# An encoder kernel whose opening runs the first gate earlier and whose queries are transposed in float32, two heads at a time

## The chip, the cores and the metric

The kernel runs on one core of a Trainium2 chip. TensorE (PE) multiplies matrices into PSUM banks, VectorE (DVE) and ScalarE (ACT) do elementwise work, GpSimd (POOL) small parts of it, and SyncE (SP) issues the loads of the weights. The metric is the device time of one execution in microseconds (us), the median of several.

## The reference

Two layers of an encoder on 256 tokens of width 1024, in float32. Each layer is a half-step FFN, a mixing block with two attentions, and a second half-step FFN:

```python
x = x + 0.5 * swiglu(rms_norm(x, ffn1_norm[l]), ffn1_w_gate[l], ffn1_w_up[l], ffn1_w_down[l])
h = rms_norm(x, mix_norm[l])
z = h @ w_in[l]
qa, ka, va, qs, ks_, vs, zg = jnp.split(z, splits, axis=-1)
qa = rms_norm(qa.reshape(B, S, NA_HEADS, NA_HEAD_DIM), na_q_norm[l])
...
o_na = neighbourhood_attention(qa, ka, va, na_rpb[l])
...
o_sw = sliding_window_gqa(qs, ks_, vs, t5_bias, sw_sink[l])
g = jax.nn.sigmoid((zg + b_gate[l]).astype(jnp.float32)).astype(x.dtype)
merged = g[:, :, 0] * (o_na @ w_branch_na[l]) + g[:, :, 1] * (o_sw @ w_branch_sw[l])
x = x + merged @ w_out[l]
x = x + 0.5 * swiglu(rms_norm(x, ffn2_norm[l]), ffn2_w_gate[l], ffn2_w_up[l], ffn2_w_down[l])
```

where `swiglu` is `(silu(x @ w_gate) * (x @ w_up)) @ w_down` with a hidden width of 2816.

## The kernel before

**Products.** The 256 tokens are two tiles t of 128. Every float32 operand is split into a rounded part hi (wh, xh: float32r, a copy on ACT) and a rest lo (wl, xl: a subtraction on DVE); `split_to` (L183) does both. `three` (L169) then makes one product of three matmuls, hi x hi, hi x lo, lo x hi. One such step with 512 columns is the unit of the program's own clock: `tick` counts steps, and `defer` puts a piece of work into the order a given number of steps later.

**Orders.** TensorE's order is the order of the program, with the deferred pieces in between. The order of the other engines is made by a scheduler when the kernel is built. The exception is the opening: `linked` (L124) ties each ACT and DVE instruction that is emitted through it behind the one before on that engine, until `chain.clear()`. A piece of weights is one load of 512 KB into one of four buffers raw, then a split wh on ACT and wl on DVE; a buffer raw is free for the next load when wl has read it.

**Opening** (L225 to 271, once, in layer 0's first FFN). The first chunk of gate and up weights, 512 columns in four pieces, is multiplied while x is still being transposed and split, for both tiles, in the banks ps_g (tag "g", two of them). Then come squares of x for the norm (`square`, L214; after the second half of a tile, GpSimd makes rs_y from it) and the pieces of the second chunk. The gate of a chunk, Silu on ACT (sg, L453) and a product on DVE (hh, L454), reads the bank of its tile and so frees it for the next chunk. The gate of the first chunk's tiles is emitted behind the whole opening, outside of the tied order.

**Queries** (L492 to 506). `queries` norms one tile of queries: z and its square on ACT, the sums hv on DVE, the root rs_y on GpSimd, the product qn on DVE (`normed`, L479). It splits qn into qs, 8 heads of [hi | lo], 128 columns each. 16 steps later `turn` transposes the eight heads with the float32r unit matrix ident_r into two banks tp (tag "tp", two of them), and ACT copies each bank into qT (or sqT): hi in partitions 0 to 63, lo in 64 to 127. The calls are Q0 and Q1 (sliding window, tiles 0 and 1), q1 and q0 (neighbourhood). `keys` (L508) does the like for K0, K1 and k0, k1, with the same head twice in a row of kn and the split after the transposes.

**Attention** (L531 to 603). Per head, `front` multiplies scores sc, then makes the softmax: S with its minimum mx on DVE, Exp on ACT, a scaling of S by GpSimd (L571). `turn` transposes S into the one bank pt, and ACT and DVE split it into ph and pl; `back` multiplies by the values into the one bank po. These are deferred by P_LAG and V_LAG, and by MORE for single heads. The bias of a head comes from t5b (sliding window) or is made by GpSimd as b from a load t (neighbourhood, L665). The string ORDER (L47) names what is projected when, and, as a5 and the like, how many steps later a head's scores come.

## Time and profile before

| | us |
|---|---|
| median of 3 runs | 1078.03 (1077.65 to 1078.95) |
| the profiled execution | 1077.96 |
| its span in the trace | 1076.2 |
| first matmul of the second chunk, behind the opening | starts at 21.21 |
| query transposes of layer 0 | 208.75, 216.30, 227.59, 234.73 |
| query transposes of layer 1 | 740.99, 748.54, 759.84, 766.98 |

Times in the trace count from the start of the span; 1.76 us of the execution lie around it. A row of a timeline gives start, length, engine, line, operation, what is written from what, and the count where several were merged. L502 is line 502 of the kernel before.

### The profile page before, as it was taken

The numbers are of one execution on the slowest core, as the hardware profiler recorded it, in microseconds if no ns is written. First come the engines' busy times: TensorE is split into PE (matmuls) and PEld (weight loads), VectorE is DVE, ScalarE is ACT, GpSimd is POOL, SyncE is SP. The second block draws the span as 40 slices with busy tenths as digits, with TensorE's granted clock in tenths as the row PEclk, the third lists the DMA queues.
The fourth block names the chain that finished last, engine by engine and source line by source line (L and its number), as shares of the span: only waits on it lengthen the run. The fifth ranks groups of instructions, "written<-read, shape, count | busy, mean of one in ns | idle before, by whom it ended". The sixth has DMA issues, their size and how long they took to land.

```text
span 1076.2 us, 14744 instructions
## 1 busy us (share of the span) xinstructions
PE 1069.2 (99%) x5125; PEld 890.2 (83%) x5125; DVE 875.9 (81%) x1337; ACT 671.6 (62%) x1014; POOL 116.9 (11%) x118
## 2 busy tenths in 40 slices
PE   9999999999999999999999999999999999999998
PEld 6888888888888888888878888888888888888887
DVE  5688898889886768879877888988898867778795
ACT  6565754788764556565465665557877646566562
POOL 1000030243520000000000000003534000000000
PEclk9999999999999999999999999999999999999999
DMA  8667665765654667756657766648666555776562
GB/s 259 214 217 237 211 206 176 227 199 151 195 184 137 202 201 241 244 167 193 208 160 232 235 210 206 183 150 242 181 196 180 181 173 161 236 232 204 197 196 78
DMA packets 98828, 212.63 MB, mean 198 GB/s; under 512 B 7569, under 2 KB 13745, under 8 KB 98753
## 3 DMA queue, kind: packets, MB, share of 16 engines
q1 hardware_dynamic: 98560, 211.60, 62.4%
q8 instruction: 40, 0.66, 0.2%
q14 instruction: 36, 0.29, 0.1%
q0 software_dynamic: 192, 0.08, 0.1%
HBM read 210.59 MB, written 1.06 MB: 197 GB/s over the span
## 4 chain that ended last, share of the span: by engine, by line
PE 95%; DVE 2%; ACT 1%; issue 1%; DMA 0%
PE g L170 22%; PE g L172 22%; PE g L171 22%; PE acc L170 5%; PE acc L172 5%; PE acc L171 5%; PE tp L318 2%; PE sc L558 1%; PE po L593 1%; PE tp L170 1%; PE tp L172 1%; PE pt L579 1%; PE tp L171 1%; DVE wl L185 1%; PE tp L201 1%
## 5 line engine op out<-in xcount | busy, mean ns | idle before, releaser
L185 DVE TENSOR_TENSOR wl<-raw,wh 128x1024 fp32r<-128x1024 f32 x336 | 404.6, 1217 | 67.8 <-ACT wh L184 65.2
L184 ACT ACTIVATE wh<-raw 128x1024 fp32r<-128x1024 f32 x336 | 346.7, 1045 | 129.4 <-DMA raw<-in_w_gu 47.8
L170 PE MATMUL g<-wh,xh 128*128 128x512 f32 (+1 forms) x976 | 383.8, 393 | 0.8 <-DVE hh L454 0.8
L172 PE MATMUL g<-wh,xl 128*128 128x512 f32 (+1 forms) x976 | 377.8, 387 | 0.7 <-DVE xl L185 0.7
L171 PE MATMUL g<-wl,xh 128*128 128x512 f32 (+1 forms) x976 | 377.4, 387 | 0.0
L172 PEld LDWEIGHTS g<-wh,xl 128*128 128x128 f32 x976 | 183.4, 188 | 40.0 <-DVE xl L185 2.1
L170 PEld LDWEIGHTS g<-wh,xh 128*128 128x128 f32 x976 | 183.6, 188 | 33.9 <-DVE hh L454 1.2
L171 PEld LDWEIGHTS g<-wl,xh 128*128 128x128 f32 x976 | 183.7, 188 | 32.7
L453 ACT ACTIVATE sg<-g,rs_y 128x256 f32<-128x256 f32 x88 | 41.0, 466 | 91.1 <-PE g L172 78.7
L454 DVE SCALAR_TENSOR_TENSOR hh<-g,rs_y,sg 128x256 f32<-128x256 f32 x88 | 42.1, 479 | 54.0 <-ACT sg L453 53.9
L170 PE MATMUL acc<-wh,hi 128*128 128x512 f32 x180 | 71.1, 395 | 0.0
L172 PE MATMUL acc<-wh,lo 128*128 128x512 f32 x180 | 70.2, 390 | 0.0
L171 PE MATMUL acc<-wl,hi 128*128 128x512 f32 x180 | 70.1, 389 | 0.0
L176 POOL TENSOR_TENSOR rs_y<-ms,mhalf 128x1 f32<-128x1 f32 x12 | 6.7, 554 | 553.5 <-DVE ms L222 545.1
L350 DVE TENSOR_TENSOR u<-raw 128x512 f32<-128x512 f32 x64 | 41.9, 685 | 15.2 <-DMA raw<-in_w_d 15.0
L184 ACT ACTIVATE corner<-raw 128x512 fp32r<-128x512 f32 x32 | 20.2, 631 | 50.1 <-DMA raw<-in_w_d 33.0
L571 POOL TENSOR_TENSOR S<-S,sm 128x512 f32<-128x512 f32 x32 | 37.1, 1160 | 65.7 <-DVE sm L570 38.3
L172 PEld LDWEIGHTS acc<-wh,lo 128*128 128x128 f32 x180 | 33.8, 188 | 7.2
L171 PEld LDWEIGHTS acc<-wl,hi 128*128 128x128 f32 x180 | 33.8, 188 | 6.8
L170 PEld LDWEIGHTS acc<-wh,hi 128*128 128x128 f32 x180 | 33.8, 188 | 6.7
L564 ACT ACTIVATE S<-S,mx 128x256 f32<-128x256 f32 x64 | 31.9, 500 | 8.0 <-DVE mx L561 7.9
L185 DVE TENSOR_TENSOR lo<-a,hi 128x896 fp32r<-128x896 f32 x32 | 33.8, 1084 | 0.5 <-ACT hi L184 0.5
(189 smaller groups left out, 1510.4 us busy)
## 6 DMA issues: line engine op xcount, KB each, us to landing
raw<-in_w_gu SPq DMA_DIRECT2D x176, 512.0 KB, 4.2
raw<-in_w_d SPq DMA_DIRECT2D x100, 512.0 KB, 4.0
raw<-in_w_in SPq DMA_DIRECT2D x64, 512.0 KB, 4.5
raw<-in_w_out SPq DMA_DIRECT2D x16, 512.0 KB, 3.6
bb<-in_b_gate SPq DMA_DIRECT2D x16, 256.0 KB, 3.6
raw<-in_w_bsw SPq DMA_DIRECT2D x8, 512.0 KB, 3.9
raw<-in_w_bna SPq DMA_DIRECT2D x8, 512.0 KB, 3.5
raw<-in_w_d SPq DMA_DIRECT2D x12, 256.0 KB, 2.6
```

Of the source, the lines that this page charges most:

```text
L170: nc.tensor.matmul(ps, xh, wh, start=first, stop=False)
L171: nc.tensor.matmul(ps, xh, wl, start=False, stop=False)
L172: nc.tensor.matmul(ps, xl, wh, start=False, stop=last)
L184: linked("act", lambda: nc.scalar.activation(hi, src, AF.Copy))
L185: linked("dve", lambda: nc.vector.tensor_tensor(lo, src, hi.bitcast(F32), ALU.subtract))
L201: nc.tensor.transpose(tp[:, i, :], xs[t][:, k * P:(k + 1) * P], ident)
L318: nc.tensor.transpose(tp[:, SLOT[t][i], :], hh[:, t, i * P:(i + 1) * P], ident)
L350: sub = lambda to, x, y: nc.vector.tensor_tensor(to, x, y, ALU.subtract)
L453: nc.scalar.activation(sg, ps[:, :FC], AF.Silu, scale=rstd[t])
L454: nc.vector.scalar_tensor_tensor(pair[:, t], ps[:, FC:], rstd[t], sg, op0=ALU.mult, op1=ALU.mult)
L564: nc.scalar.activation(S_[:, t, :], S_[:, t, :], AF.Exp, bias=mx[:, t:t + 1], scale=-1.0, accum_out=sm[:, t:t + 1])
L571: nc.gpsimd.tensor_tensor(S_, S_, sm.unsqueeze(2).to_broadcast([P, T, S]), ALU.mult)
```

## The change

Three edits, and constants that go with them.

1. **Opening.** The steps of the first chunk's last three pieces are emitted before the second chunk's pieces. The gate of tile 0 goes through `linked` (new function `glu`), behind the first half square of tile 1 and ahead of the second piece of the second chunk. The second half square comes behind that piece.
2. **Queries.** qn is no longer split before the transposes. It is transposed in float32 with ident, two heads at a time: four transposes instead of eight, into one bank. The split follows, on each half of the partitions apart (e = 0, 1): ACT writes hi, DVE writes lo into the other half of the partitions, so that qT has hi and lo of a head above each other, and for odd heads the other way round. ident_r goes. qn lies in the buffers that qs had.
3. **Lags.** K1's transposes come 1 step later, k0's 1.5, the transposes of S of head 4 of the sliding window 3 later instead of 1.5, and the first head's scores 6 steps later instead of 5.

```diff
@@ -43,8 +43,8 @@
 LAG = 3
 H_LAG, NORM_LAG, QK_LAG, P_LAG, V_LAG, M_LAG = 7.9, 4.0, 16, 10, 7.5, 5.5
 LAST_LAG = 6.1
-MORE = {"Q1": 2, ("sw", 4): 1.5, ("na", 4): 2, ("na", 5): 1.5}
-ORDER = ("Q0 Q1 K0 K1 q1 q0 a5 k0 a5 k1 a3 v0 a1 a5 v1 a3 g0 a1 a5 g1 a4 g2 a0 g3 a0 a4 g4 a1 a5 g5 a4 "
+MORE = {"Q1": 2, "K1": 1, "k0": 1.5, ("sw", 4): 3, ("na", 4): 2, ("na", 5): 1.5}
+ORDER = ("Q0 Q1 K0 K1 q1 q0 a6 k0 a5 k1 a3 v0 a1 a5 v1 a3 g0 a1 a5 g1 a4 g2 a0 g3 a0 a4 g4 a1 a5 g5 a4 "
          "g6 a0 g7")
 FMAX = 3.0e38
 IN_W = 4352
@@ -87,8 +87,6 @@
 
     ident = const.tile([P, P], F32, name="ident")
     make_identity(nc, ident)
-    ident_r = const.tile([P, P], F32R, name="ident_r")
-    nc.vector.tensor_copy(ident_r, ident)
     mhalf = const.tile([P, 8], F32, name="mhalf")
     nc.vector.memset(mhalf, -0.5)
     warm = const.tile([P, 1], F32, name="warm")
@@ -222,7 +220,7 @@
             nc.vector.tensor_scalar(v, v, 1.0 / D, EPS, op0=ALU.mult, op1=ALU.add)
             rstd[t] = rsqrt(v, 1)
 
-    def opening(w, l):
+    def opening(w, l, early):
         def piece(i, c=0):
             return load(w[l, 2 * i * P:(2 * i + 2) * P, c * 512:(c + 1) * 512].rearrange("(k p) n -> p k n", p=P),
                         2, 512)
@@ -258,14 +256,16 @@
         pieces.append(piece(3))
         square(0, 0, idle)
         square(0, 1, idle)
-        second = [piece(i, 1) for i in range(2)]
+        for i in (1, 2, 3):
+            for t in range(T):
+                steps(t, i)
+        second = [piece(0, 1)]
         square(1, 0, idle)
+        early(ps[0])
+        second.append(piece(1, 1))
         square(1, 1, idle)
         second += [piece(i, 1) for i in range(2, KD // 2)]
         chain.clear()
-        for i in (1, 2, 3):
-            for t in range(T):
-                steps(t, i)
         defer(24, "constants", constants)
         defer(70, "scaled", scaled)
         return ps, second
@@ -434,11 +434,20 @@
 
                 return rest
 
+            def glu(t, ps, pair):
+                if t == 0:
+                    pair[0] = act.tile([P, T, FC], F32, name="hh", tag="xg", bufs=2)
+                sg = fp.tile([P, FC], F32, name="sg", tag="sg", bufs=2)
+                linked("act", lambda: nc.scalar.activation(sg, ps[:, :FC], AF.Silu, scale=rstd[t]))
+                linked("dve", lambda: nc.vector.scalar_tensor_tensor(pair[0][:, t], ps[:, FC:], rstd[t], sg,
+                                                                     op0=ALU.mult, op1=ALU.mult))
+
             waiting = []
             for c in range(NFC):
                 first = n == 0 and c == 0
+                pair = [None]
                 if first:
-                    both, second = opening(w_gu, l)
+                    both, second = opening(w_gu, l, lambda ps: glu(0, ps, pair))
                 elif n == 0 and c == 1:
                     pieces = second
                 else:
@@ -446,13 +455,12 @@
                 prep = PREP if n else PREP_FIRST
                 if c in prep:
                     prepare(prep[c])
-                pair = act.tile([P, T, FC], F32, name="hh", tag="xg", bufs=2)
                 for t in range(T):
-                    ps = both[t] if first else project(t, pieces, 512)
-                    sg = fp.tile([P, FC], F32, name="sg", tag="sg", bufs=2)
-                    nc.scalar.activation(sg, ps[:, :FC], AF.Silu, scale=rstd[t])
-                    nc.vector.scalar_tensor_tensor(pair[:, t], ps[:, FC:], rstd[t], sg, op0=ALU.mult, op1=ALU.mult)
-                waiting.append((c, pair))
+                    if not first:
+                        glu(t, project(t, pieces, 512), pair)
+                    elif t:
+                        glu(t, both[t], pair)
+                waiting.append((c, pair[0]))
                 if c % 2 or c >= NFC - 3:
                     defer(LAST_LAG if c == NFC - 1 else H_LAG, ("h", c), lambda group=waiting: turn(group))
                     waiting = []
@@ -490,18 +498,17 @@
                                         r.unsqueeze(2).to_broadcast([P, nh, DH]), ALU.mult)
 
             def queries(key, ps, t, qT):
-                qn = act.tile([P, NH, DH], F32, name="qn", tag="xg", bufs=2)
+                qn = mp.tile([P, 2, NH, DH], F32, name="qn", tag="qk", bufs=2)[:, 0]
                 normed(ps, t, NH, qn)
-                qs = mp.tile([P, NH, 2, DH], F32R, name="qs", tag="qk", bufs=2)
-                split_to(qs[:, :, 0, :], qs[:, :, 1, :], qn)
 
                 def turn():
-                    for half in range(2):
-                        tp = ps_tp.tile([P, 4, P], F32R, name="tp", tag="tp")
-                        for j in range(4):
-                            nc.tensor.transpose(tp[:, j, :], qs[:, 4 * half + j].rearrange("p two d -> p (two d)"),
-                                                ident_r)
-                        nc.scalar.activation(qT[:, 4 * half:4 * half + 4, t * P:(t + 1) * P], flipped(tp), AF.Copy)
+                    tp = ps_tp.tile([P, 4, P], F32, name="tp", tag="tp")
+                    for j in range(4):
+                        nc.tensor.transpose(tp[:, j, :], qn[:, 2 * j:2 * j + 2].rearrange("p two d -> p (two d)"), ident)
+                    cols = slice(t * P, (t + 1) * P)
+                    for e in range(2):
+                        a, b = e * DH, (1 - e) * DH
+                        split_to(qT[a:a + DH, e, :, cols], qT[b:b + DH, e, :, cols], flipped(tp[a:a + DH]))
 
                 defer(QK_LAG + MORE.get(key, 0), key, turn)
 
@@ -522,7 +529,7 @@
                         nc.vector.scalar_tensor_tensor(kl[:, h0:h0 + m, t * P:(t + 1) * P], tp[:, :m, :], gk,
                                                        hi.bitcast(F32), op0=ALU.mult, op1=ALU.subtract)
 
-                defer(QK_LAG, key, turn)
+                defer(QK_LAG + MORE.get(key, 0), key, turn)
 
             def values(hi, lo, ps, t):
                 nc.scalar.activation(hi, ps, AF.Copy, scale=rstd[t])
@@ -555,7 +562,7 @@
                     sm = small.tile([P, T], F32, name="sm", tag="sm")
                     for t in range(T):
                         for i, k in enumerate((kh, kl)):
-                            nc.tensor.matmul(ps[:, t, :], qT[:, h, t * P:(t + 1) * P], k[:, kidx(h), :],
+                            nc.tensor.matmul(ps[:, t, :], qT[:, h % 2, h // 2, t * P:(t + 1) * P], k[:, kidx(h), :],
                                              start=i == 0, stop=i == 1)
                     for t in range(T):
                         nc.vector.tensor_tensor_reduce(S_[:, t, :], ps[:, t, :], b(t), -1.0, least,
@@ -606,10 +613,10 @@
                 both = mp.tile([P, 2, *shape], F32R, name=name, tag=tag)
                 return both[:, 0], both[:, 1]
 
-            sqT = mp.tile([P, NH, S], F32R, name="sqT", tag="sq")
+            sqT = mp.tile([P, 2, NH // 2, S], F32R, name="sqT", tag="sq")
             skT = pair("skT", "sk", [2, S])
             sv = mp.tile([P, T, 2, 3 * DH], F32R, name="sv")
-            qT = mp.tile([P, NH, S], F32R, name="qT")
+            qT = mp.tile([P, 2, NH // 2, S], F32R, name="qT")
             kT = (mp.tile([P, NH, S], F32R, name="kh", tag="kh"), mp.tile([P, NH, S], F32R, name="kl"))
             va = mp.tile([P, T, NH, P], F32R, name="va")
             oB = pair("oB", "oB", [4, T, P])
```

**How the orders move.** First place: DVE in the opening, from the sums ms of tile 0 on. Before:

```order
L221 TENSOR_TENSOR ms<-ssq 128x1
L222 TENSOR_SCALAR ms<-ms 128x1
L185 TENSOR_TENSOR wl<-raw,wh 128x1024 x2
L454 SCALAR_TENSOR_TENSOR hh<-g,rs_y,sg 128x256
L221 TENSOR_TENSOR ms<-ssq 128x1
L222 TENSOR_SCALAR ms<-ms 128x1
L185 TENSOR_TENSOR wl<-raw,wh 128x1024 x2
L454 SCALAR_TENSOR_TENSOR hh<-g,rs_y,sg 128x256
```

And with the change:

```order
L219 TENSOR_TENSOR ms<-ssq 128x1
L220 TENSOR_SCALAR ms<-ms 128x1
L183 TENSOR_TENSOR wl<-raw,wh 128x1024
L442 SCALAR_TENSOR_TENSOR hh<-g,rs_y,sg 128x256
L183 TENSOR_TENSOR wl<-raw,wh 128x1024
L219 TENSOR_TENSOR ms<-ssq 128x1
L220 TENSOR_SCALAR ms<-ms 128x1
L183 TENSOR_TENSOR wl<-raw,wh 128x1024 x3
L442 SCALAR_TENSOR_TENSOR hh<-g,rs_y,sg 128x256
```

The gate hh of tile 0 stands behind one weight split instead of two; between it and that of tile 1 stand four splits instead of two, the last of which is the first piece of the third chunk. ACT's order (wh, sg) moves in the same way.

Second place: TensorE in layer 0's attention, where the last query call (q0) and the S of the first head are transposed. Before:

```order
L579 MATMUL pt<-ident,S 128x128 x4
L170 MATMUL g<-wh,xh_1793 128x512
L171 MATMUL g<-wl,xh_1793 128x512
L172 MATMUL g<-wh,xl_1794 128x512
L502 MATMUL tp<-ident_r,qs 128x128 x8
L170 MATMUL g<-wh,xh_1737 128x512
```

And with the change:

```order
L170 MATMUL g<-wh,xl_1792 128x512
L168 MATMUL g<-wh,xh_1791 128x512
L169 MATMUL g<-wl,xh_1791 128x512
L170 MATMUL g<-wh,xl_1792 128x512
L507 MATMUL tp<-ident,qn 128x128 x4
L586 MATMUL pt<-ident,S 128x128 x4
L168 MATMUL g<-wh,xh_1735 128x512
```

The eight transposes of the query call are four, and stand one step earlier against pt, directly ahead of it.

Some steps later the S of the second head is transposed. Before:

```order
L593 MATMUL po<-ph,sv 128x256
L593 MATMUL po<-pl,sv 128x256
L593 MATMUL po<-ph,sv 128x256
L593 MATMUL po<-pl,sv 128x256
L579 MATMUL pt<-ident,S 128x128 x4
L170 MATMUL g<-wh,xh_1737 128x512
L171 MATMUL g<-wl,xh_1737 128x512
L172 MATMUL g<-wh,xl_1738 128x512
```

And with the change:

```order
L586 MATMUL pt<-ident,S 128x128 x4
L168 MATMUL g<-wh,xh_1735 128x512
L169 MATMUL g<-wl,xh_1735 128x512
L170 MATMUL g<-wh,xl_1736 128x512
L600 MATMUL po<-ph,sv 128x256
L600 MATMUL po<-pl,sv 128x256
L600 MATMUL po<-ph,sv 128x256
L600 MATMUL po<-pl,sv 128x256
```

The products po of the first head, which stood ahead of this pt, stand a step behind it.

Third place: DVE in the same stretch, between the qn of the last query call and the lo part pl of the first head. Before, behind qn:

```order
L486 TENSOR_REDUCE hv<-sq 128x8
L487 TENSOR_SCALAR hv<-hv 128x8
L185 TENSOR_TENSOR wl<-raw,wh 128x1024
L185 TENSOR_TENSOR qs<-qn,qs 128x8x64
L561 ISA S,mx<-sc,t5b,nsnk 128x256
L561 ISA mx 128x1
L561 ISA S,mx<-sc,t5b,nsnk 128x256
L561 ISA mx 128x1
L185 TENSOR_TENSOR wl<-raw,wh 128x1024
L489 TENSOR_TENSOR kn<-z,rs_y 128x8x64
L185 TENSOR_TENSOR wl<-raw,wh 128x1024
L185 TENSOR_TENSOR pl<-pt,ph 128x512
```

With the change, first the part from qn to the next scores:

```order
L497 TENSOR_TENSOR qn<-z,rs_y 128x512
L183 TENSOR_TENSOR qT<-tp,qT 64x4x128
L494 TENSOR_REDUCE hv<-sq 128x8
L183 TENSOR_TENSOR wl<-raw,wh 128x1024
L495 TENSOR_SCALAR hv<-hv 128x8
L183 TENSOR_TENSOR qT<-tp,qT 64x4x128
L568 ISA S,mx<-sc,t5b,nsnk 128x256
L568 ISA mx 128x1
L568 ISA S,mx<-sc,t5b,nsnk 128x256
L568 ISA mx 128x1
```

and then the part up to pl:

```order
L183 TENSOR_TENSOR wl<-raw,wh 128x1024 x2
L497 TENSOR_TENSOR kn<-z,rs_y 128x8x64
L576 TENSOR_TENSOR sm<-sm,es 128x2
L183 TENSOR_TENSOR wl<-raw,wh 128x1024
L577 RECIPROCAL sm<-sm 128x2
L183 TENSOR_TENSOR qT<-tp,qT 64x4x128
L568 ISA S,mx<-sc,t5b,nsnk 128x256
L568 ISA mx 128x1
L568 ISA S,mx<-sc,t5b,nsnk 128x256
L568 ISA mx 128x1
L183 TENSOR_TENSOR pl<-pt,ph 128x512
L494 TENSOR_REDUCE hv<-sq 128x8
```

Three query parts, one more weight split and the scores of one more head stand ahead of pl; behind it come the sum hv, the last query part and two small rows ahead of the rest of hv, from which GpSimd makes the next rs_y.

## The prediction

> **What bounds the kernel now.** I read the page first: the shares of the engines and, in its fourth part, the chain of work that ended last.
>
> ```profile
> span 1076.2 us, 14744 instructions
> ...
> PE 1069.2 (99%) x5125; PEld 890.2 (83%) x5125; DVE 875.9 (81%) x1337; ACT 671.6 (62%) x1014; POOL 116.9 (11%) x118
> ...
> PE 95%; DVE 2%; ACT 1%; issue 1%; DMA 0%
> ```
>
> TensorE is busy for 99% of the span and is 95% of the chain. Its order is fixed by hand, so time can leave the kernel in two ways only: fewer or shorter matmuls, or a shorter wait of TensorE. Next I asked for all of its waits.
>
> ```profile
> PE idle L120 <- DVE blank L115: 1.6, 1, 1.6
> PE g L170 <- DVE hh L454: 0.8, 1, 0.8
> PE g L172 <- DVE xl L185: 0.7, 1, 0.7
> ```
>
> The first is the start of the program and the third is the start of layer 1's first FFN; the change touches neither. The second, 0.8 us in the opening, is one that it aims at. So the whole prize is this wait and what the query transposes cost on TensorE. Last I looked at the stretch of attention that is reordered, in the view by windows: length, then busy time (and instructions) of TensorE, its weight loads, VectorE, ScalarE and GpSimd, then granted clock, DMA share and GB/s.
>
> ```profile
> 203.00:252.00 49.00, 49.00 (x287) 42.42 (x287) 43.08 (x83) 42.85 (x83) 22.39 (x20) 1.00 0.67 205
> ```
>
> Here TensorE never stops, and VectorE (DVE) and ScalarE (ACT) are busy for 43 of 49 us each. The granted clock is 1.00. Whatever is given to VectorE here finds little room.
>
> The profiled execution took 1077.96 us around a span of 1076.2, and stands 0.07 under the median of the runs, 1078.03. The sum is made against 1077.96. A measurement of this kernel can tell a change of about 0.2%, that is 2.2 us: faster means below 1075.9, slower above 1080.2.
>
> **Part 1: query transposes on TensorE.** Eight calls in all (two token tiles, two kinds of queries, two layers).
>
> ```profile
> 208.75 0.64 PE tp L502 x8
> ...
> 233.60 0.44 PE pt L579 x4
> ...
> 234.73 0.65 PE tp L502 x8
> 235.38 0.31 PE g L170
> ...
> 238.01 0.23 PE g L170
> ...
> 240.77 0.47 PE po L593 x4
> ```
>
> These are pieces of the chain: start, length, what. Eight float32r transposes hold TensorE for 0.64 us. Four float32 transposes of the same size (L579, those of the attention weights) hold it for 0.44. So each call saves 0.20 us, 1.6 in all. Once a layer the four of a query call now stand directly ahead of a pt group; two groups of small transposes then share one return to the weight matmuls. Such a return costs 0.08: the first matmul behind a query call takes 0.31, one behind scores 0.23. I take 0.85 us a layer, 1.7 in all; bounds 1.5 and 1.8.
>
> **Part 2: the splits move behind the transposes.** Before, a call had one hi part and one lo part of 128x512 on the queries, and two ACT copies out of the banks. Now it has two hi parts on ACT and two lo parts on DVE, each of 64 partitions by 4x128. ACT loses one instruction a call; DVE gains one.
>
> ```profile
> L185 DVE TENSOR_TENSOR lo<-tp,hi 128x512 fp32r<-128x512 f32 x12 | 8.2, 682 | 0.1
> ...
> L598 DVE TENSOR_TENSOR o<-o,po 64x256 f32<-64x256 f32 x32 | 13.3, 415 | 3.8 <-ACT o L597 3.2
> L561 DVE CUSTOM_DVE_ANT_0 S<-sc,b 128x256 f32<-128x256 f32 x32 | 12.1, 414 | 0.2
> ```
>
> No row has a 64-partition tensor_tensor of 512 columns. The nearest are the two of 256 columns: 415 ns on 64 partitions, 414 on 128. So half the partitions save nothing, and a 64x512 lo costs what lo<-tp,hi does: 682 ns, of which 0.60 is the step to the next start (the qs at 231.98 below, the next row at 232.59). DVE then has 0.6 us more per call, 2.4 per layer. The lower bound is no extra time, if two halves cost one whole; I take 0.6, the value by the rows. The Trainium skill, page "VectorE: DVE Perf Modes", section "Why `tensor_reduce` can't reduce along partition axis", says that each of the 128 partition lanes is a pipeline of its own along the free dimension; by that rule two halves take twice the time of one whole, which is against this change, and the trace agrees (415 against 414 ns). Were the time in proportion to the partitions instead, DVE would have nothing more to do, the two waits worked out below would not come, and the sum would be 1075.9 in place of 1077.6.
>
> What does this extra hide behind? Up to 228.6 us behind DVE's idle time; after that behind nothing:
>
> ```profile
> 228.61 1.52 DVE L489 TENSOR_TENSOR qn<-z,rs_y 128x512 f32<-128x512 f32 x1 [0.59 <-POOL rs_y L176]
> 230.05 0.67 DVE L486 TENSOR_REDUCE hv<-sq 128x8 f32<-128x512 f32 x1
> ...
> 230.84 1.22 DVE L185 TENSOR_TENSOR wl<-raw,wh 128x1024 fp32r<-128x1024 f32 x1
> 231.98 0.69 DVE L185 TENSOR_TENSOR qs<-qn,qs 128x512 fp32r<-128x512 f32 x1
> 232.59 0.47 DVE L561 CUSTOM_DVE_ANT_0 S<-sc,t5b,nsnk 128x256 f32<-128x256 f32 x1
> ...
> 233.40 1.22 DVE L185 TENSOR_TENSOR wl<-raw,wh 128x1024 fp32r<-128x1024 f32 x1
> ...
> 236.27 0.68 DVE L185 TENSOR_TENSOR pl<-pt,ph 128x512 fp32r<-128x512 f32 x1
> ...
> 241.09 0.60 PE L579 MATMUL pt<-ident,S 128*128 128x128 f32 x4
> ```
>
> The timeline of DVE, with start, length and, in brackets, the idle time ahead; the last row is TensorE's. The qn of the last query call waits for GpSimd until 228.6. From there the steps from start to start are 1.44 for qn, about 0.7 for hv, 1.14 for a weight split wl, 0.81 for a pair of score rows S and 0.61 for a 512-column row. The new order (the third piece above) puts these between qn and the end of pl, that is, of the lo part of the first head's attention weights: qn 1.44, three query parts qT 1.8, hv 0.7, four wl 4.56, two pairs S 1.62, kn 0.61, pl 0.61, four small ones about 0.3. Together 11.6: pl ends at **240.2**. Before, pl had started at 236.27 and was over 4 us early.
>
> The next pt (second head) writes the one bank that pl reads. Before, TensorE got there at 241.09, behind a po of 0.47. Now po stands behind it, and TensorE is 0.85 ahead: it arrives at 241.09 - 0.47 - 0.85 = 239.8. **A new wait of 0.4 to 0.5** takes the place of half of the gain. Queued behind the waiting pt is all of TensorE's order.
>
> **Part 3: what is late next.** GpSimd, whose hv comes from the same DVE row of work.
>
> ```profile
> 239.46 1.04 POOL L571 TENSOR_TENSOR S<-S,sm 128x512 f32<-128x512 f32 x1 [2.63 <-ACT S L564]
> 240.66 1.64 POOL L176 TENSOR_TENSOR rs_y<-hv,mhalf 128x8 f32<-128x8 f32 x1 [0.17 <-DVE sm L569]
> 242.27 2.79 POOL L665 TENSOR_TENSOR b<-t,mask 128x512 f32<-128x512 f32 x2
> 245.02 1.03 POOL L571 TENSOR_TENSOR S<-S,sm 128x512 f32<-128x512 f32 x1
> ...
> 247.00 0.60 PE L579 MATMUL pt<-ident,S 128*128 128x128 f32 x4
> ...
> L665 POOL TENSOR_TENSOR b<-t,mask 128x512 f32<-128x512 f32 x16 | 23.3, 1461 | 16.0 <-DVE mx L561 15.7
> ```
>
> The order on GpSimd stays: rs_y, two b, then the third head's S. In the new DVE order hv's row (0.7), the last qT part (0.6) and two small rows stand behind pl, so hv is ready at 240.2 + 1.4 = 241.6 and rs_y starts 0.95 later than at 240.66. S then ends at 246.05 + 0.95 = 247.0. TensorE reaches the third pt at 247.00 - 0.85 + 0.45 = 246.6 and waits 0.4. At 247.0 it stands where it stood before: **nothing of the layer's 0.85 is left.** Layer 1 has the same order, so I take 0 for both layers. The bounds are 0.85 kept a layer (no backlog) and 0.6 lost (DVE 0.6 later than walked, one query part). The later steps of this stretch are the same instructions in the same order. The keys moved 1 and 1.5 steps later and the scores moved 1 step later cost nothing by themselves: TensorE runs the same matmuls in another order, and the moved ones have more time for their inputs. That is also what covers the longer way of the queries through ACT, DVE, ACT, DVE before the first scores. On SP's queue two t5b loads move ahead of the loads t that feed b; the row of b, all calls together, waits for DVE and for no load, so I cost that at nothing; without that cover b, and with it S, would be late by what the load lacks.
>
> **Part 4: the opening.** Rows of ACT, DVE and TensorE.
>
> ```profile
> 17.32 1.99 ACT L184 ACTIVATE wh<-raw 128x1024 fp32r<-128x1024 f32 x2
> 19.22 0.57 ACT L217 ACTIVATE idle<-x 128x512 f32<-128x512 f32 x1
> ...
> 19.83 0.46 ACT L453 ACTIVATE sg<-g,rs_y 128x256 f32<-128x256 f32 x1
> ...
> 23.95 1.06 ACT L184 ACTIVATE wh<-raw 128x1024 fp32r<-128x1024 f32 x1 [0.79 <-DMA raw<-in_w_gu]
> ...
> 18.40 2.36 DVE L185 TENSOR_TENSOR wl<-raw,wh 128x1024 fp32r<-128x1024 f32 x2 [0.60 <-ACT wh L184]
> 20.68 0.48 DVE L454 SCALAR_TENSOR_TENSOR hh<-g,rs_y,sg 128x256 f32<-128x256 f32 x1
> ...
> 19.83 0.61 PE L237 MATMUL g<-wl,xh 128*128 128x512 f32 x2
> ...
> 21.21 0.50 PE L170 MATMUL g<-wh,xh 128*128 128x512 f32 x1 [0.77 <-DVE hh L454]
> ...
> 26.78 0.39 PE L170 MATMUL g<-wh,xh 128*128 128x512 f32 x1
> ```
>
> The gate of the first tile (sg, hh) frees the bank for the second chunk. Now one weight split instead of two stands ahead of it: the square moves from 19.22 to about 18.3, sg ends near 19.6, hh near 20.1. The last pair of opening matmuls starts at 19.83; with two steps of 0.23 the next could start at 20.28. So the wait goes and 21.21 becomes 20.28: **0.93 gained there.** What is late next is the gate of the second tile. Before, two splits stood ahead of it, now three. The third is that of the chunk after, whose load lands at 23.95 by the ACT row, which was idle for it. From there: wh 1.06, then wl 1.18 (half of 2.36), then hh 0.48: done at 26.7. TensorE wants that bank 24 matmuls later, at 26.78 - 0.93 = 25.85, and so waits 0.85; if the load lands 0.6 sooner, 0.25. Left are **0.1 to 0.7; I take 0.35**, near the row.
>
> **The sum:** 1077.96 - 2 x 0.85 + 2 x 0.85 - 0.35 = 1077.6.
>
> **The rivals.** (a) *The cover holds.* If DVE has slack that the walk does not see (weight splits that come later, or two half parts at the price of one), the waits at pt do not come: 1.7 kept, and the opening keeps 0.35 to 0.93. That gives 1077.96 - 1.7 - 0.93 = 1075.3 at best, 1075.9 with 0.35. For it speaks that pl was 4 us early before; against it, 43 of 49 us busy. (b) *Half is given back*: the wait at pt comes, but the one for GpSimd does not, or only one layer shows both. Then about 0.85 of the 1.7 is kept: 1077.96 - 0.85 - 0.35 = 1076.8, or 1076.4 with 0.7 from the opening, within 0.2%. For it: the walk adds up 20 rows, and a single weight split less ahead of pl takes the first wait away. (c) *DVE becomes the bound, and it is slower.*
>
> ```profile
> L185 DVE TENSOR_TENSOR wl<-raw,wh 128x1024 fp32r<-128x1024 f32 x336 | 404.6, 1217 | 67.8 <-ACT wh L184 65.2
> ```
>
> Place: the pt bank and GpSimd's S behind DVE, as in parts 2 and 3. Each us that DVE is later than in my walk delays TensorE by that us, in both layers. The walk lets every lo part start at once, but each waits for its hi part on ACT, and the second hi part for the first lo part. Where DVE waits for ACT's hi today, in the weight splits of this page row, it stands idle 65.2 us over 336, or 0.2 each. Four query parts lie between 228.6 and GpSimd's rs_y: 0.8. And the hv that releases the walk's start has four lo parts ahead of it where three qs stood, 0.6 more if DVE's idle time ahead doesn't take it. Together 1.4: 1077.96 + 2 x 1.4 - 0.35 = 1080.4. It decides from 1.3 us on. For it: DVE is 88% busy. Against: both pieces have to come whole, in both layers.
>
> **How the numbers follow.** Forecast 1077.6 with its own range 1076.6 to 1078.8: 0.46. Rival (b): 0.20, within 0.2% too. Rival (a): 0.22, faster in most of it. Rival (c): 0.12, with 0.10 beyond 0.2%. So faster 0.21, same 0.69, slower 0.10. The range of 8 in 10 goes from 1075.3, the best that all terms give, to 1079.8, where DVE is 1.1 us late in both layers.
>
> **What would show it.** In the changed kernel's waits of TensorE: no wait for hh at 20 us, but one for hh (or a weight split) near 26, of 0.25 to 0.85; and new waits of 0.3 to 0.6 us at pt near 240 (for DVE's pl) and 246 (for GpSimd's S), and the same in layer 1's attention. In the chain a query call of 4 at 0.44. The forecast is wrong if pt waits nowhere (rival a), or if one of these waits exceeds 1.3 us (rival c); the price of a split is wrong if a 64x4x128 lo part takes far from 0.68 us.

## The result, and the profile after

| | us |
|---|---|
| after, median of 4 runs | 1084.89 (1084.39 to 1085.77) |
| before, median of 4 runs beside it | 1077.85 (1077.65 to 1078.95) |
| ratio | 1.0063, 95% interval 1.0051 to 1.0075 |
| profiled execution after, and its span | 1084.99, 1083.2 |

The changed kernel is 7.0 us slower, outside the predicted range (1075.3 to 1079.8). The page of the changed kernel, with the span, the engines and the chain by engine:

```profile
span 1083.2 us, 14667 instructions
...
PE 1068.2 (99%) x5093; PEld 887.2 (82%) x5093; DVE 885.1 (82%) x1344; ACT 669.2 (62%) x1006; POOL 120.6 (11%) x118
...
PE 85%; DVE 7%; DMA 2%; issue 2%; ACT 2%; POOL 1%; SPq 0%; DVEq 0%; ACTq 0%; POOLq 0%
```

TensorE's work is 1.0 us less, as intended, but it is 85% of the chain where it was 95%. The rest are stretches in which it waited. Its waits after the change (released by, us in total, times, longest):

```profile
PE pt L586 <- POOL S L578: 3.2, 2, 1.8
PE pt L586 <- DVE pl L183: 2.5, 2, 1.2
PE idle L118 <- DVE blank L113: 1.6, 1, 1.6
PE pt L586 <- DVE sm L577: 1.4, 2, 0.7
PE tp L199 <- DMA x<-in_x: 1.0, 1, 1.0
PE g L170 <- DVE xl L183: 0.7, 1, 0.7
PE tp L168 <- DVE lo L183: 0.5, 1, 0.5
PE sc L565 <- DVE skT L529: 0.4, 2, 0.2
PE g L168 <- DVE hh L442: 0.2, 1, 0.2
```

Four are new and come twice, once a layer: pt for GpSimd's S, for DVE's pl and for DVE's sm, together 7.1 us, and the scores sc for the keys' skT, 0.4. The wait for hh has shrunk from 0.8 to 0.2. The wait for x lies at the start and costs nothing: at 13.6 us TensorE is 0.08 ahead of the kernel before. The wait for lo comes once, at 145 us. To see where time goes, I set the same weight matmul of both kernels side by side and subtract the start times: negative is a lead of the changed kernel. At the second chunk's first matmul the difference is -1.03, behind the gate of tile 1 -0.39, and -0.26 up to 142 us; behind the wait for lo it is +0.2. In layer 0's attention it goes from -0.53 (at 234 us) to +0.83 (245), +2.91 (248) and +3.81 (264), and in layer 1 from +2.79 (757) to +7.05 (800). So nothing of the opening's gain is left when the attention begins, and each attention loses some 3.5 us. The timeline of attention in layer 0: TensorE's pt groups, the DVE rows behind which they wait, and GpSimd (start, length, engine, line; the idle time ahead in brackets):

```profile
241.49 0.63 PE L586 MATMUL pt<-ident,S 128*128 128x128 f32 x4 [1.23 <-DVE pl L183]
...
266.82 0.63 PE L586 MATMUL pt<-ident,S 128*128 128x128 f32 x4 [0.70 <-DVE sm L577]
...
229.12 1.52 DVE L497 TENSOR_TENSOR qn<-z,rs_y 128x512 f32<-128x512 f32 x1 [0.59 <-POOL rs_y L174]
...
240.66 0.68 DVE L183 TENSOR_TENSOR pl<-pt,ph 128x512 fp32r<-128x512 f32 x1
...
242.77 0.17 DVE L495 TENSOR_SCALAR hv<-hv 128x8 f32<-128x8 f32 x1
...
243.43 1.64 POOL L174 TENSOR_TENSOR rs_y<-hv,mhalf 128x8 f32<-128x8 f32 x1 [2.94 <-DMA raw<-in_w_in]
245.03 2.79 POOL L672 TENSOR_TENSOR b<-t,mask 128x512 f32<-128x512 f32 x2
247.78 2.02 POOL L578 TENSOR_TENSOR S<-S,sm 128x512 f32<-128x512 f32 x1
```

From qn on, DVE's timeline shows no idle time until 251 us. The first pl ends at 241.34 and the pt behind it starts 0.15 later. The hv row ends at 242.94, GpSimd's rs_y starts at 243.43, and S, which had ended at 246.05, ends at 249.80: the third pt starts at 249.86 in place of 247.00. How full the engine is, in the windows view of 229 to 260 us (length; busy time of TensorE, weight loads, DVE, ACT, GpSimd), first before, then after:

```profile
229.00:260.00 31.00, 31.00 (x177) 26.62 (x177) 29.02 (x63) 25.59 (x57) 14.72 (x12) 1.00 0.62 177
```

```profile
229.00:260.00 31.00, 27.99 (x157) 23.50 (x156) 30.53 (x62) 24.45 (x53) 15.09 (x12) 1.00 0.59 165
```

DVE goes from 29.0 to 30.5 of 31 us, with one row fewer, and TensorE does 20 matmuls fewer in the same time: this fits a DVE that sets the pace here, and the experiments test it.

### The profile page after: what moved, and what is told of

Its sections match the earlier page's. It is cut to its first block, busy times and chain, and to the rows that moved or that the text cites. A ratio compares the mean times of both kernels' runs of the same rounds, so it can differ in the third digit from the quotient of the medians.

```text
span 1083.2 us, 14667 instructions
## 1 busy us (share of the span) xinstructions
PE 1068.2 (99%) x5093; PEld 887.2 (82%) x5093; DVE 885.1 (82%) x1344; ACT 669.2 (62%) x1006; POOL 120.6 (11%) x118
## 4 chain that ended last, share of the span: by engine, by line
PE 85%; DVE 7%; DMA 2%; issue 2%; ACT 2%; POOL 1%; SPq 0%; DVEq 0%; ACTq 0%; POOLq 0%
PE g L170 19%; PE g L168 19%; PE g L169 19%; PE acc L170 5%; PE acc L168 5%; PE acc L169 5%; DVE wl L183 3%; PE tp L318 2%; PE tp L168 1%; PE tp L170 1%; PE tp L169 1%; PE po L600 1%; DMA raw<-in_w_d 1%; PE pt L586 1%; PE sc L565 1%
```

## The experiments

"Before" beside a time is the kernel before on the same chip. In every variant the scheduler makes a new order for the engines other than TensorE, so a single difference can hold some of that too. In the expectations, theory L blames the lags, D the time on DVE, H the hand-overs between ACT and DVE. Heads are counted from 0 where they have a number: head 2 is the third.

### Which of the three edits costs

Four kernels. `e1_opening_only` is the kernel before with edit 1 alone; `e2_no_opening` the changed kernel without it. `e3_lags_only` is the kernel before with edit 3 alone, and `e4_old_lags` is e2 with the lags of before, so edit 2 alone.

```diff
 e3 (against before):
-MORE = {"Q1": 2, ("sw", 4): 1.5, ("na", 4): 2, ("na", 5): 1.5}
+MORE = {"Q1": 2, "K1": 1, "k0": 1.5, ("sw", 4): 3, ("na", 4): 2, ("na", 5): 1.5}
-ORDER = ("... q0 a5 k0 ...
+ORDER = ("... q0 a6 k0 ...
 e4 (against e2): the same lines the other way round
```

> The kernel before with the opening edit alone. All theories: within 0.3 us of before (about 1077.9). In the changed kernel the opening is 0.28 us ahead when the second chunk runs, and 0.19 us late at 145 us, where the loads of the down weights set the pace. If the opening had a part in the loss, this kernel would be 1 us or more slower than before.

> The changed kernel with the old opening: queries and lags alone. All three theories of the attention put the whole loss here: 1084.4 to 1085.2. Against them: 1083.5 or less, if the opening's shift of the loads feeds the loss.

> The kernel before with the new lags alone (K1, k0, head 4, first scores). Theory L (the new order of TensorE makes the waits at pt): 1081 to 1085. Theory D (more time on DVE) and theory H (hand-overs between ACT and DVE in the split): 1077.0 to 1079.0.

> The changed queries with the old lags and the old opening. Theory L: 1076.5 to 1079. Theories D and H: 1083 to 1087, and no better than with the new lags, since the same 2.4 us more of DVE and the same hand-overs a layer are there and the first scores come a step earlier.

| | median | before | ratio (95%) |
|---|---|---|---|
| e1, opening | 1077.81 | 1078.24 | 0.9996 (0.9988 to 1.0005) |
| e2, queries and lags | 1085.30 | 1078.24 | 1.0066 (1.0053 to 1.0079) |
| e3, lags | 1081.21 | 1078.24 | 1.0027 (1.0017 to 1.0037) |
| e4, queries | 1081.63 | 1078.24 | 1.0029 (1.0018 to 1.0040) |

The opening has no part in the loss. The lags alone cost 3.0 and the queries alone 3.4, together 6.4 of e2's 7.1. So e1 to e3 came as theory L had them, e2 0.1 above its range, but e4 lies between the two forecasts, and no theory holds alone. New waits of TensorE at pt in e3, first, and at tp and pt in e4:

```profile
PE pt L579 <- DVE sm L570: 1.4, 2, 0.7
...
PE pt L579 <- POOL S L571: 0.4, 2, 0.2
```

```profile
PE tp L516 <- DVE qT L183: 1.2, 2, 0.6
PE pt L576 <- POOL S L568: 1.1, 2, 0.7
PE tp L516 <- DVE skT L519: 1.0, 2, 0.5
```

The sm wait belongs to the lags. With the old lags the queries show it elsewhere: the keys' transposes (tp) now wait for a bank that the query split (qT) or the other keys' split (skT) still reads.

### Which lag

`e10_sw4_alone` has head 4's lag alone, `e11_other_lags` the rest of edit 3; `e9_sw4_back` is e2 with head 4's lag put back.

```diff
 e10 (against before), e9 the other way round (against e2):
-("sw", 4): 1.5
+("sw", 4): 3
```

> The kernel before with only head 4's lag at 3 in place of 1.5. Theory S: a wait of 0.7 at pt near 264 us in each layer, 1079.4 to 1080.8. Rival (the loss of the lags comes from K1, k0 and the first scores): 1077.7 to 1078.6.

> The kernel before with the new lags of K1, k0 and the first scores, and head 4's old one. Theory S: 1077.7 to 1079.2. Rival: 1080 to 1081.5.

> The changed queries and lags, old opening, but head 4 of the sliding window keeps its 1.5. Theory S (the transposes of head 4 now stand 1.5 steps nearer to those of head 5, which write the same bank, and those wait for head 4's lo part): the wait of 0.7 near 266 us and the one in layer 1 go, 1082.6 to 1083.8. Rival: another wait takes their place, 1084.5 to 1086.

e10: 1080.09 against 1078.16, 1.0019 (1.0010 to 1.0028). e11: 1079.71 against 1078.16, 1.0014 (1.0006 to 1.0023). e9: 1084.04 against 1078.16, 1.0052 (1.0039 to 1.0064). So head 4 costs 1.9 and the others 1.5 on the kernel before; on the changed queries e9 takes back 1.3. Only e10 came as forecast: e11 and e9 lie between theory S and its rival, and in e9 the wait for sm goes while that for S grows from 3.2 to 3.5. The timeline around it, pt groups of heads 4 and 5, then ACT's ph and DVE's pl of head 4, first in the kernel before:

```profile
258.89 0.60 PE L579 MATMUL pt<-ident,S 128*128 128x128 f32 x4
...
263.04 0.60 PE L579 MATMUL pt<-ident,S 128*128 128x128 f32 x4
...
260.13 0.60 ACT L184 ACTIVATE ph<-pt 128x512 fp32r<-128x512 f32 x1
...
260.91 0.69 DVE L185 TENSOR_TENSOR pl<-pt,ph 128x512 fp32r<-128x512 f32 x1
```

and then in e10:

```profile
260.23 0.60 PE L579 MATMUL pt<-ident,S 128*128 128x128 f32 x4
...
264.08 0.63 PE L579 MATMUL pt<-ident,S 128*128 128x128 f32 x4 [0.71 <-DVE sm L570]
...
262.61 0.60 ACT L184 ACTIVATE ph<-pt 128x512 fp32r<-128x512 f32 x1
...
263.24 0.69 DVE L185 TENSOR_TENSOR pl<-pt,ph 128x512 fp32r<-128x512 f32 x1
```

There is one bank pt. Head 4's group comes 1.3 us later, head 5's stands where it stood. In that 1.3 us ACT has taken up other work, so ph comes 2.5 later, pl ends at 263.93 instead of 261.60, and head 5 starts 0.15 behind it: the same 0.15 as behind pl at 241.34 above. The profile names sm, a row that ended a moment later; the row whose data the bank holds is pl. This wait, 0.71 a layer, is 1.4 of the 1.9.

Of the other lags' 1.5, 0.4 is a wait for S at pt. Another 0.7 lies in the first scores, whose weights are the keys skT. TensorE's scores and DVE's skT in the kernel before:

```profile
224.88 0.64 PE L558 MATMUL sc<-skT,sqT 128*128 128x256 f32 x4
...
224.24 0.48 DVE L522 SCALAR_TENSOR_TENSOR skT<-tp,qkg,skT 128x256 fp32r<-128x256 f32 x1
```

and in e11, with the weight loads (PEld):

```profile
225.36 1.00 PE L558 MATMUL sc<-skT,sqT 128*128 128x256 f32 x4
...
225.74 0.42 PEld L558 LDWEIGHTS sc<-skT,sqT 128*128 128x128 f32 x3 [0.42 <-DVE skT L522]
...
225.22 0.47 DVE L522 SCALAR_TENSOR_TENSOR skT<-tp,qkg,skT 128x256 fp32r<-128x256 f32 x1
```

The scores and K1's transposes come 0.48 later, but skT comes 0.98 later: on DVE the rows qs (224.02) and hv (224.62), which stood behind it, now stand ahead of it. The group holds TensorE for 0.84 instead of 0.48 (the next matmul starts at 226.20 and 225.36), and for 0.85 instead of 0.47 in layer 1. The wait falls inside a merged row, so the list of TensorE's waits does not name it.

### How much DVE time the stretch can take

Two kernels add work to the kernel before: one row of 128x512 from the bank per query call, whose result nobody reads, or two. Two take work out: in `e6_less_dve` (from e2) and `e17_less_dve_old_lags` (from e4) ACT writes the odd heads' lo part as a plain copy, so that this rest is not computed, and DVE has as many query rows as before. In the edit, src is flipped(tp[a:a + DH]).

```diff
 e5 (against before; e18 has the second line twice):
+extra = mp.tile([P, 4, P], F32, name="extra", tag="extra")
+nc.vector.tensor_tensor(extra, tp.bitcast(F32), qT[:, 4:8, t * P:(t + 1) * P].bitcast(F32), ALU.subtract)
 e6, e17, for e = 1:
-split_to(qT[a:a + DH, e, :, cols], qT[b:b + DH, e, :, cols], flipped(tp[a:a + DH]))
+nc.scalar.activation(qT[a:a + DH, e, :, cols], src, AF.Copy)
+nc.scalar.activation(qT[b:b + DH, e, :, cols], src, AF.Copy)
```

> The kernel before with one more DVE row of 128x512 a query call, that reads the second bank of transposes once ACT has copied it; its result is not used. DVE gets 0.6 us a call more, as in the changed kernel, and no hand-over from DVE back to ACT. Theory D: 1081 to 1086. Theory H: 1077.5 to 1079.5.

> The kernel before with two more DVE rows of 128x512 a query call in place of one; their result is not used. One row a call fitted into the slack of 0.59 us that pt had near 241 and took 0.53 of it. If DVE's time counts from there on, two rows cost 0.6 to 1.5 us a layer: 1079.3 to 1081.5. If DVE's time does not matter by itself, 1077.8 to 1078.8.

> The changed queries and lags, old opening, but the lo part of the odd heads is an ACT copy of the transposes in place of the subtraction, so the lo part of these heads is not computed. DVE is back at the load of the kernel before; ACT still waits for DVE once a call. Theory D: 1077 to 1079.5. Theory H: 1081 to 1084, as the wait of ACT for the first lo part stays.

> The changed queries with the old lags and the old opening, but the lo part of the odd heads is an ACT copy in place of the subtraction, so the lo part of these heads is not computed; DVE is back at the load of the kernel before. If DVE's time is what turns the shorter transposes into waits, the 1.7 us of TensorE come through and it beats both kernels: 1076.0 to 1077.8. If the longer hold of the bank of transposes does it (ACT, DVE, ACT in turn), 1080 to 1082 as with the whole split.

| | median | before | ratio (95%) |
|---|---|---|---|
| e5, one row a call more | 1078.41 | 1078.45 | 1.0001 (0.9992 to 1.0010) |
| e18, two rows a call more | 1081.48 | 1078.16 | 1.0032 (1.0021 to 1.0043) |
| e6, e2 with one row a call less | 1081.11 | 1078.45 | 1.0027 (1.0017 to 1.0037) |
| e17, e4 with one row a call less | 1079.48 | 1078.16 | 1.0014 (1.0005 to 1.0022) |

The first row a call is free, the second costs 3.3 us over the eight calls. In the kernel before, S of the second and third head ends 0.59 and 0.94 us ahead of its pt (240.50 for 241.09, and 246.05 for 247.00); in e5 0.06 and 0.41 are left. So the cover is about one row of 0.6 us. New waits of e18, and its window of 229 to 260 us:

```profile
PE pt L582 <- POOL S L574: 1.4, 3, 0.6
...
PE tp L522 <- POOL kn L514: 0.7, 1, 0.7
```

```profile
229.00:260.00 31.00, 30.25 (x169) 25.50 (x168) 30.08 (x64) 25.70 (x57) 15.89 (x12) 1.00 0.60 172
```

DVE is busy 30.1 us here, 30.5 in the changed kernel. In e5 and e18 the rows at the start of the stretch keep the order of the kernel before, so this pair is the cleanest test of DVE's time. e6 comes down to e3: with the new lags, the whole cost of the queries, 4.1 (e2 less e3), goes. With the old lags 2.1 of 3.4 go (e4 less e17 by the medians); e17 keeps a wait of the keys' transposes for skT, 1.5 us over both layers, and 0.9 for S at pt. By the forecasts, e5 came as theory H had it, e18 at the upper end of the range in which DVE's time counts; e6 lies in theory H's range, which leaves out what the lags cost, and e17 between its two. ACT's wait for DVE's lo of the even heads stays in e6, 6.0 us in all:

```profile
L503 ACT ACTIVATE sqT<-tp 64x512 fp32r<-64x512 f32 x4 | 2.4, 595 | 4.3 <-DVE sqT L183 4.2
L503 ACT ACTIVATE qT<-tp 64x512 fp32r<-64x512 f32 x4 | 2.4, 594 | 1.9 <-DVE qT L183 1.8
```

So the loss can go without the hand-over going. The next pair takes the hand-over away and leaves DVE's rows.

### The hand-over between ACT and DVE

In the change ACT writes hi of the even heads, DVE their lo, then ACT hi of the odd heads, DVE their lo. The groups of these rows in the changed kernel (busy, mean ns | idle time ahead, and what ended it):

```profile
L183 DVE TENSOR_TENSOR qT<-tp,qT 64x512 fp32r<-64x512 f32 x8 | 5.5, 689 | 0.2
L182 ACT ACTIVATE sqT<-tp 64x512 fp32r<-64x512 f32 x8 | 4.7, 587 | 5.0 <-DVE sqT L183 5.0
L182 ACT ACTIVATE qT<-tp 64x512 fp32r<-64x512 f32 x8 | 4.7, 584 | 3.2 <-DVE qT L183 3.2
```

ACT stands idle 8.2 us in front of these rows, until DVE's lo of the first half is done. `e7_his_first` (from e2) and `e8_his_first_old_lags` (from e4) write both hi first.

```diff
+for e in range(2):
+    a = e * DH
+    nc.scalar.activation(qT[a:a + DH, e, :, cols], flipped(tp[a:a + DH]), AF.Copy)
 for e in range(2):
     a, b = e * DH, (1 - e) * DH
-    split_to(qT[a:a + DH, e, :, cols], qT[b:b + DH, e, :, cols], flipped(tp[a:a + DH]))
+    nc.vector.tensor_tensor(qT[b:b + DH, e, :, cols], flipped(tp[a:a + DH]),
+                            qT[a:a + DH, e, :, cols].bitcast(F32), ALU.subtract)
```

> The changed queries and lags, old opening, with both hi parts of a call on ACT first and then both lo parts on DVE. DVE has the same time as in the changed kernel; ACT no longer waits for DVE. Theory D: 1083 to 1085.5. Theory H: 1076.5 to 1079.5.

> The changed queries with both hi parts first, the old lags, the old opening. If the loss is the sum of two parts, the hand-overs (3 us: the difference of the two kernels with the new lags) and the lags (3 us), this kernel keeps the shorter transposes: 1076.2 to 1078.6. If the two parts are not additive, because DVE is also short of time, it stays above 1079.5.

e7: 1082.37 against 1078.45, 1.0037 (1.0025 to 1.0050), 2.9 less than e2. e8: 1081.79 against 1078.16, 1.0032 (1.0020 to 1.0044), no better than e4. Waits at pt of e7, then of e8:

```profile
PE pt L580 <- DVE pl L183: 2.1, 2, 1.1
PE pt L580 <- DVE sm L571: 1.8, 2, 1.1
```

```profile
PE pt L580 <- POOL S L572: 3.1, 4, 1.1
```

With the new lags the wait for S is gone and 2.9 of the 4.1 come back, less than theory H and more than theory D had. With the old lags nothing comes back, as the second forecast of e8 has it: the keys' waits of e4 go, and the wait for S grows from 1.1 to 3.1. In front of the rows of q1 and q0 ACT waits 3.2 us in e2, but 0.3 in e4, so with the old lags there was little hand-over to win at this place.

The two parts can't be told apart by adding: 4.1 goes with the row (e6), 2.9 with the hand-over (e7), and both come out of the same 4.1. There is a rival for both. DVE's order at the start of the stretch differs: in e2, e4 and e8, as in the kernel before, the hv of the last query call stands behind the S of the first scores; in e6, e7 and e17 the scheduler has put it ahead. The last qn, in e2 and then in e7:

```profile
229.48 1.52 DVE L487 TENSOR_TENSOR qn<-z,rs_y 128x512 f32<-128x512 f32 x1 [0.59 <-POOL rs_y L174]
```

```profile
227.29 0.69 DVE L487 TENSOR_TENSOR qn<-z,rs_y 128x512 f32<-128x512 f32 x1 [0.28 <-POOL rs_y L174]
```

It ends 3.0 us earlier, of which 0.7 is e2's later arrival at the attention (at 209 us). In e7 GpSimd also does one b instead of two ahead of the third head's S. Of e6, e7, e8 and e17, the three that gained are those with the early hv. So it is shown that the queries' split makes DVE and GpSimd late; which share of that the row, the hand-over and this order have is not shown, as the order changed along with the edits.

### GpSimd's order

In `e14_changed_late_b` (from e2) and `e13_old_lags_late_b` (from e8) the two b are issued behind the S of head 3 on GpSimd, the fourth head. `e15_sw4_back_his_first_late_b` is e14 with both hi first and head 4's lag put back.

```diff
+with tc.issue_after(scaled_S["sw", 3].ins):
     nc.gpsimd.tensor_tensor(b, src, mask[:, None, None, :].to_broadcast([P, T, ROWS, GW]), ALU.add)
```

> The changed queries and lags, old opening, with GpSimd's first two b put behind S of head 3, so that they no longer stand between rs_y and S of head 2. Theory Q (S of head 2 waits in GpSimd's queue: in the changed kernel its sums are ready at 243.0 and it starts at 247.8, behind rs_y and two b): the wait of 1.8 us at pt near 250 goes in both layers, 1081 to 1082.5. Rival (S is late because DVE is late, whatever GpSimd does first): 1084.5 to 1086.

> The changed queries with both hi parts first, old lags, old opening, and the two b put behind S of head 3. Theory Q: S of heads 2 and 3 start earlier, the waits near 248 and 255 us go (3.1 us in all): 1077.5 to 1079.5. Rival: unchanged, 1081 to 1082.5, if DVE's weight splits and GpSimd's rows only block each other at another place.

> The changed queries with both hi parts first, the new lags of K1, k0 and the first scores, head 4's old lag, old opening, and the late b. If the parts add up (3 less from the hand-overs, 1.3 to 1.9 less from head 4, and up to 0.5 a layer from b): 1078.5 to 1080.5. Below 1077.6 it would beat both kernels; that needs the wait of 1.0 us at pt for DVE's pl near 241 to go too, which nothing here touches.

All against 1078.37. e14: 1083.42, 1.0049 (1.0035 to 1.0062). e13: 1081.39, 1.0029 (1.0018 to 1.0041). e15: 1081.80, 1.0034 (1.0022 to 1.0047). The wait for S, 3.2 us in e2, is gone in e14, yet only 1.9 us come back: DVE has the same work, and a row of the values (va) is now late for a weight matmul. e13 gains little on e8, 0.4 by the medians: the wait for S falls from 3.1 to 1.0, and one of 1.6 for va comes, as its rival had it. e14 lies between its forecasts, and e15 misses its own (1078.5 to 1080.5): the parts do not add up. TensorE's waits in e14:

```profile
PE pt L576 <- DVE pl L183: 2.5, 2, 1.2
...
PE pt L576 <- DVE sm L567: 1.4, 2, 0.7
PE g L168 <- DVE va L526: 1.2, 2, 0.6
```

No variant beat the kernel before; e1 (1077.81) can't be told from it.

## Why the prediction was wrong

**Part 1, the transposes: right.** A query call holds TensorE for 0.44 (208.93 us) and 0.45 (216.23). The lead of TensorE grows by 0.25 to 0.33 at a call, a little more than the 0.20 to 0.21 that the prediction took.

**Part 2, the price of a split: right.** 689 ns on 64 partitions, against 682 forecast: half the partitions save nothing.

**Part 2 and 3, the walk of DVE and GpSimd: the right places, too small.** This is the first step that failed.

| | predicted | measured |
|---|---|---|
| start of the walk, qn | 228.61 | 229.12 |
| first pl ends | 240.2 | 241.3 |
| wait at the second pt | 0.4 to 0.5 | 1.23 |
| TensorE reaches the second pt | 239.8 | 240.26 |
| rs_y starts | 241.6 | 243.43 |
| third S ends | 247.0 | 249.80 |
| wait at the third pt | 0.4 | 1.78 |

pl has the rows ahead of it that the walk gave it. It is 1.1 late because the walk starts 0.5 later and because 12.1 us in place of 11.6 pass from qn on. The late start comes through the first scores: hv stands behind their S, and they start 0.33 later and wait for skT. From pl to the end of hv 1.7 us pass instead of 1.4; rs_y starts another 0.5 behind hv, for which the profile names a load (not followed up); and S itself takes 2.02 instead of 1.03. In layer 1 rs_y starts 0.14 behind hv, and the wait at the third pt is 1.42. The prediction set the queries' loss against their gain and got 0; by the runs they cost 3.4 us with the old lags and 4.1 with the new (shown), the saved 0.85 a layer already taken off. With the new lags all of it goes with DVE's row (e6) and 2.9 of it with the hand-over, hi of the second half waiting for lo of the first (e7), which the prediction counted only in rival (c) and at 0.8 a layer; as the order of DVE's rows changed in both, the shares stay open. e5 and e18 show how thin the cover was: one row of 0.6 us a call is free, the second costs 3.3. The forecast itself had DVE late for the two pt; what it missed is how much later DVE and GpSimd would be, at several places and in both layers.

**Part 3, "the keys moved 1 and 1.5 steps later and the scores moved 1 step later cost nothing by themselves": wrong.** This is the second step that failed. Alone, the lags cost 3.0 (e3). The prediction's bounds left the term out, and of head 4's pt it spoke nowhere: it costs 1.9 (e10). "More time for their inputs" was false for the first scores: they move by 0.48, their keys skT by 0.98, and that costs 0.7 in both layers (e11). And it looked at one side only; the other side is the next user of the bank. That "the later steps of this stretch are the same instructions in the same order" was false for this head. Of the 1.5 of the other lags (e11), these 0.7 and 0.4 of waits for S at pt are seen; the last 0.4 is not explained.

**Part 4, the opening: right at its place, but not kept.** The first matmul of the second chunk leads by 1.03, the lead behind tile 1's gate is 0.39, and 0.27 to 0.29 in the matmuls that follow; 0.35 was forecast. The chain of the changed kernel goes there through the load of the next chunk's first piece, its wh and its wl, as the prediction has it. Of the 1.03, 0.64 is given back by then: 0.21 in the wait for hh, the rest in smaller stalls ahead of it. The sum carries the 0.35 to the end. In the changed kernel it is gone at 145 us, where TensorE waits 0.51 for lo; in e1, whose profile has no such wait, 0.10 is left at the end, and its time can't be told from before.

**The rivals.** (c), "DVE becomes the bound", named the place, the mechanism and the sign, and its mark, a wait of more than 1.3, came (1.78). It held DVE 1.4 us late and gave 1080.4; what came was S 2.8 later than walked in layer 0, and the lags on top. (a) and (b) fall: the waits at pt come in both layers, and nothing of the layers' gain is kept.

**Still open.** With the old lags 1.3 of the queries' 3.4 us stay when DVE has no more to do than before (e17). The wait for the keys' bank is seen, but not isolated. The saving on TensorE, 1.7 us, doesn't show in the time of any variant. Whether both hi first gives 2.9 with the new lags and nothing with the old because of ACT's wait (3.2 against 0.3) or because of the early hv is not settled.

## What to carry to other kernels

Saved time on the busiest engine moves all its deadlines forward: before crediting it, list for each row that it waits on how early that row is now, and spend added work of the feeding engines against that slack in that stretch (here 0.6 us), not against their idle share of the span. A row that is moved later also moves closer to the next user of its bank, and falls behind other work of the engines that empty the bank; that end has to be checked too. The rows that feed a moved row can fall behind other work too. Where one wait is taken away in such a stretch the next late row takes its place, so the gain is at most the distance to it. And where a scheduler orders the feeding engines anew for every variant, compare their orders before a difference is put down to the edit.

## What the runs showed of the hardware

Two rows of the changed kernel that took far longer than usual lie beside GpSimd. DVE's timeline from 245.7 us on, to be read beside GpSimd's rows above (b until 247.82, S from 247.78 to 249.80):

```profile
245.70 1.07 DVE L497 TENSOR_TENSOR kn<-z,rs_y 128x512 f32<-128x512 f32 x1
246.69 2.21 DVE L183 TENSOR_TENSOR wl<-raw,wh 128x1024 fp32r<-128x1024 f32 x1
248.83 0.99 DVE L576 TENSOR_TENSOR sm<-sm,es 128x2 f32<-128x2 f32 x1
```

wl takes 1.22 elsewhere, sm 0.15 and S 1.03. If only one of the two engines can go at a time, the ends fit: wl does its 1.1 after b (247.82 to 248.90), S its 1.0 after wl (to 249.80), and sm ends right after S (249.82). The Trainium skill, page "SBUF — State Buffer", section "Who interferes with whom", states it: a DVE instruction with two inputs in SBUF contends with a GpSimd instruction that reads SBUF, and the ports that they share are an exclusive lock. The trace agrees, with some 1.0 us on either engine, and so does pl at 243.08, which reads one input from PSUM and keeps its 0.69 beside rs_y. The kernel before has such rows too: wl at 248.98 takes 1.99 and qn at 228.61 takes 1.52, each beside an S; in e7, where no GpSimd row lies beside it, qn takes 0.69. The walk of the prediction did not know of it: it put S at 1.03. How much of the 7 us hangs on this overlap was not isolated.
